# Attention trunk on one core: scores of two heads in one block with alternating row halves, dilated heads weighed in pairs

## The chip, the cores and the metric

One Trainium2 chip, one of its cores. The metric is device time in microseconds (us) of one execution. Engines in the views: PE is TensorE's matmul side, PEld its weight loads, DVE VectorE, ACT ScalarE, POOL GpSimd, SP SyncE, which issues the weights' DMAs. Names like L684 are lines of the kernel before; in the changed kernel the same lines lie one to three further down.

## The reference, cut to what matters

A decoder trunk of two layers over 256 positions of width 2048, all in fp32. Layer 0 mixes with sliding-window attention (job A, 16 heads) and with three dilated patterns that are merged per position (jobs B0 and B1, 4 heads each, three patterns a head); layer 1 with stick-breaking attention (jobs C0 and C1, 8 heads each) and latent attention (jobs D0 and D1, 8 heads each). An MLP of width 8192 follows in each layer.

```python
# A and B, per head (B: for each of three patterns)
scores = einsum(q, k) * (1 / sqrt(64)) - slope * distance     # masked
p = exp(scores - max(scores)); out = (p @ v) / sum(p)
# C, per head: strictly causal, no softmax
z = einsum(q, k) * scale
after = reverse_cumsum(log_keep) - log_keep
out = exp(log_beta + after) @ v
# D, per head: 64 + 32 = 96 numbers in q and k
s = (einsum(q_nope, k_nope) + einsum(q_rope, k_rope)) * scale
out = softmax(s) @ v
```

## The kernel before, in words

**Big matmuls.** All projections and MLP products run on PE with weights that stream from HBM in units of 128 x 1024 (`Stream`). Each unit is split into a high and a low part: ACT casts `w_hi` (L120), DVE subtracts to get `w_lo` (L121). Three units are split ahead of their use. `ws` (L325, L326) holds the weights in the array, `as_` (L371 to L373) the activations.

**Attention between them.** After each unit of weights `pump` runs one step of the attention (`attn_step`), so a step's small matmuls stand in PE's queue as one block between two runs of big ones. The order is written out: `todo` lists the scores still to be made, `due` what later steps must do, `flips` the transposes. In a step come first what is due (weighing, then the flip, then later stages), then one new score if the list and the buffers allow it.

One head of a job goes through these stages:

- *score* (step i): `qk` makes the scores of 256 positions in two matmuls, 128 x 128 (L684) and 128 x 256 (L685), into a PSUM tile `sc`, of which there are two, one bank each. A, B and C heads have 64 numbers, so q and k lie on 64 partitions: even heads on 0 to 63, odd ones on 64 to 127. D heads lie on partitions 0 to 95. In the same step the job's first stage runs on DVE and frees `sc`: bias and row maxima in A, B and D (L767, L808, L1024, then L699), the mask in C (L1043).
- *later stages*, a step apart: in A, B and D the exponentials on ACT and the division on DVE; in C three functions on ACT, sums on DVE (L1054, two scans L1057, L1058) and the exponential on ACT.
- *flip*: three transposes on PE (L259) and a copy to SBUF as `pT` on ACT, one head and pattern a step.
- *weigh*, two steps later: `v` times `pT` into the PSUM tile `o` (L278, L280). A head writes 64 of the 128 partitions of `o`, odd heads the upper half. In A, C and D two heads are weighed together, with their matmuls alternating; in B each head and pattern by itself. After both heads `y` is made on ACT and DVE (L284, L285).

Every job's heads are scored one a step, each pattern of B by itself, in a list that grows as the projections finish.

Of the kernel before, what the change touches and what calls it, by code (L numbers as in the profile page):

```python
# [11 lines left out]
F32 = mybir.dt.float32  # L12
# [6 lines left out]
P = 128  # L19
S = 256  # L20
# [143 lines left out]
class Trunk:  # L164
    def __init__(self, tc, ctx, args):
        self.tc = tc
        self.nc = tc.nc
        self.a = args
        self.split_ahead = 3
        self.dma_ahead = 5  # L170
        pool = lambda name, bufs, **kw: ctx.enter_context(tc.tile_pool(name=name, bufs=bufs, **kw))
        self.const = pool("const", 1)
        self.raw = pool("raw", 6)
        self.spl = pool("spl", 4)
        self.res = pool("res", 1)
        self.small = pool("small", 5)
        self.ps = pool("ps", 1, space=bass.MemoryType.PSUM)
        self.w = Stream(self)
        self.side = deque()
        self.late = deque()  # L180
        self.todo = deque()
        self.due = {}
        self.flips = deque()
        self.s_live = 0
        self.i = 0


    def pump(self):
# [15 lines left out]

    def queue(self, job, u=None):

        if u is None:
            self.todo.extend((job, h, 0) for h in range(job.n))
        else:
            self.todo.extend((job, h, u) for h in range(job.n))  # L210

    def at_step(self, i, prio, fn, *args):
        self.due.setdefault(i, []).append((prio, len(self.due.get(i, ())), fn, args))
# [1 line left out]
    def attn_step(self):  # L215
        i = self.i
        self.i += 1
        if self.flips and self.flips[0][0] <= i:
            _, job, h, u = self.flips.popleft()
            self.at_step(i, 2, self.flip, job, h, u)  # L220
            if job.per > 1:
                self.at_step(i + 2, 1, self.weigh, job, (h,), u)
            elif h % 2:
                self.at_step(i + 2, 1, self.weigh, job, (h - 1, h), 0)
        for _, _, fn, args in sorted(self.due.pop(i, []), key=lambda t: t[:2]):
            fn(*args)
        if not self.todo:
            return
        job, h, u = self.todo[0]
        per = job.per  # L230
        if h not in job.s:
            if self.s_live == self.s_bufs:
                return
            self.s_live += 1
            if per > 1:
                job.s[h] = self.at.tile([P, per * 384], F32, name="S", bufs=self.s_bufs)
            else:
                pair = self.at.tile([P, 768], F32, name="S", bufs=self.s_bufs)
                job.s[h], job.s[h + 1] = pair[:, 0:384], pair[:, 384:768]
        self.todo.popleft()  # L240
        sc = self.ps.tile([P, 384], F32, name="sc", bufs=2)
        job.score(h, u, sc)
        job.stages[0](h, u, sc, job.s[h])
        if u == per - 1:
            for n, fn in enumerate(job.stages[1:]):
                self.at_step(i + 1 + n, 3, fn, h, job.s[h])
            self.flips.extend((i + job.lag, job, h, v) for v in range(per))

    def finish(self, job):
        while job.left:  # L250
# [427 lines left out]
            one(t, 3, mv, r)  # L678


    def qk(self, sc, q, k):

        nc = self.nc
        nc.tensor.matmul(sc[:, 0:P], q[:, 0:P], k[:, 0:P], start=True, stop=True, skip_group_check=True)  # L684
        nc.tensor.matmul(sc[:, P:384], q[:, P:S], k, start=True, stop=True, skip_group_check=True)  # L685

    def softmax(self, per, scale=1.0, sink=None):

# [44 lines left out]
    def even(self):  # L733
        nc = self.nc
        slopes = alibi(16)
        qa = self.project(512, scale=0.125) + self.project(512, scale=0.125)
        kd = self.tile2()
        va = self.tile2()
        kvf = self.at.tile([P, 2, S], F32, name="kvf", bufs=1)
        vf = kvf[:, 1, :]  # L740

        def take(f, bank):
            self.join(kvf[:, f, :], bank)
            if f == 0:
                for kv in range(2):
                    for half in range(2):
                        eng = nc.scalar.copy if half else nc.vector.tensor_copy
                        eng(kd[half * HD:half * HD + HD, kv, :], kvf[kv * HD:kv * HD + HD, 0, :])

        self.ws(self.xT, KT, 256, take)  # L750
        self.pump()

        def flip_v():
            pt = self.ps.tile([P, 384], F32, name="pt")
            for t in range(2):
                nc.tensor.transpose(pt[:, t * P:(t + 1) * P], vf[:, t * P:(t + 1) * P], self.ident)
            nc.vector.tensor_copy(va[:, :, 0:P], pt[:, 0:S].rearrange("p (t c) -> p t c", t=2))

        self.at_step(self.i, 0, flip_v)
        top, power, divide = self.softmax(1, sink=lambda h: self.sinks[:, h:h + 1])  # L760

        def score(h, u, sc):
            r = slice((h % 2) * HD, (h % 2) * HD + HD)
            self.qk(sc, qa[h // 4][r, (h // 2) % 2, :], kd[r, h // 8, :])

        def bias(h, u, sc, st):
            nc.vector.scalar_tensor_tensor(st, self.masks[:, 0, :], -slopes[h], sc, op0=ALU.mult, op1=ALU.add)  # L767
            top(h, st)

        def value(h, u, blk):  # L770
            return va[:, blk, (h // 8) * HD:(h // 8) * HD + HD]

        ja = Job("A", 16, 1, score, (bias, power, divide), value, 5, self.y_at)
        self.queue(ja)
        jb = [self.even_b(0, self.y_at), self.even_b(1, self.x_slot)]
        self.finish(jb[0])
        self.finish_side()
        ys = ja.out + jb[0].out
        st = self.new_stats()

        def rest():
            self.finish(jb[1])
            yield jb[1].out

        late = LazyTiles(rest())
        late.tiles += ys
        for c in range(3):
            o = self.as_(late if c == 2 else ys, 12 if c == 2 else 10, 512)
            self.add_res(o, c, True, st if c == 2 else None)
            self.pump()  # L790
        for c in range(2):
            o = self.as_(jb[1].out, 2, 512)
            self.add_res(o, c, False, st)
        o = self.as_(late, 12, 512, hold=2)
        return (o, 3, True), st

    def even_b(self, half, y):
        nc = self.nc
        sl = alibi(8)
        qkv = []  # L800
        top, power, divide = self.softmax(3)

        def score(h, u, sc):
            r = slice((h % 2) * HD, (h % 2) * HD + HD)
            self.qk(sc, qkv[u][0][r, h // 2, :], qkv[u][1][r, h // 2, :])

        def bias(h, u, sc, st):
            nc.vector.scalar_tensor_tensor(st[:, u * 384:(u + 1) * 384], self.masks[:, 1 + u, :], -sl[half * 4 + h], sc,  # L808
                                           op0=ALU.mult, op1=ALU.add)
            if u == 2:  # L810
                top(h, st)

        def value(h, u, blk):
            return qkv[u][2][:, blk, h * HD:h * HD + HD]

        job = Job(f"B{half}", 4, 3, score, (bias, power, divide), value, 4, y)
        for gi in range(3):
            q = self.project(256, scale=0.125)[0]
            k = self.project(256)[0]
            qkv.append((q, k, None))  # L820
            self.queue(job, gi)
            o = self.as_(self.xT, KT, 256)
            v = self.tile2()
            for t in range(2):
                nc.scalar.copy(v[:, t, :], o[t])
            self.pump()
            qkv[gi] = (q, k, v)
        return job
# [186 lines left out]
    def job_d(self, name, qs, kv, y):  # L1015
        nc = self.nc
        ks, vs = kv
        top, power, divide = self.softmax(1, scale=1.0 / math.sqrt(96))

        def score(h, u, sc):  # L1020
            self.qk(sc, qs[h // 2][0:96, h % 2, :], ks[h // 2][0:96, h % 2, :])

        def bias(h, u, sc, st):
            nc.vector.tensor_tensor(st, self.masks[:, 1, :], sc, op=ALU.add)  # L1024
            top(h, st)

        def value(h, u, blk):
            return vs[h // 4][:, blk, (h % 4) * HD:(h % 4) * HD + HD]

        job = Job(name, 8, 1, score, (bias, power, divide), value, 5, y)  # L1030
        self.queue(job)
        return job

    def job_c(self, name, qs, ks, vs, y):
        nc = self.nc
        kept = {}

        def score(h, u, sc):
            r = slice((h % 2) * HD, (h % 2) * HD + HD)
            self.qk(sc, qs[h // 4][r, (h // 2) % 2, :], ks[h // 4][r, (h // 2) % 2, :])  # L1040

        def mask(h, u, sc, st):
            nc.vector.tensor_tensor(st, self.masks[:, 0, :], sc, op=ALU.add)  # L1043
# [22 lines left out]
        job = Job(name, 8, 1, score, (mask, soft, sums, power), value, 6, y)  # L1066
# [98 lines left out]
```

## Time and profile before

| | before |
|---|---|
| median of 3 runs | 2243.89 us (2241.61 to 2249.12) |
| the profiled execution | 2248.41 us, span 2246.6 us |
| PE busy | 2216.6 us (99%) |
| DVE busy | 1406.8 us (63%) |
| ACT busy | 1060.7 us (47%) |
| mean granted clock of TensorE | 0.996 |

A busy time is the union of an engine's instructions. PE's instructions overlap, so the distance between two starts tells what one of them costs the engine, not the duration of a row. An fp32 matmul appears as two passes, each with its own weight load.

### The profile page before, as it was taken

Reading aid. Unit: us, or ns where it says so; the run is one execution under the profiler, and the core shown is the slowest. Engines: PE = TensorE matmul, PEld = TensorE weight load, DVE = VectorE, ACT = ScalarE, POOL = GpSimd, SP = SyncE. Lnnn points to the kernel's source line nnn. Section 1 sums busy time; section 2 is a strip of 40 time slices with the busy share of each in tenths; the row PEclk is TensorE's granted clock in tenths of the full one; section 3 lists DMA queues with packets and bytes.
Section 4 is the critical chain, followed back from the end, with each engine's and each line's share of the span. In section 5 each row is a group of like instructions: output and inputs, shape, how many; then the busy total and the mean of one; then the engine's idle time right before and its main releaser. Section 6 shows DMA issues by size and latency. Waiting matters only on the chain.

```text
span 2246.6 us, 30036 instructions
## 1 busy us (share of the span) xinstructions
PE 2216.6 (99%) x11604; PEld 1847.6 (82%) x11604; DVE 1406.8 (63%) x1903; ACT 1060.7 (47%) x1525; POOL 62.0 (3%) x85
## 2 busy tenths in 40 slices
PE   9999999999999999999999999999999999999997
PEld 7878887788888888888878887778888888888885
DVE  5766355776556456556567887978555655554655
ACT  4554344454345345345344575635434534444542
POOL 0000000000000000000003201000000000000001
PEclk9999999999999999999999999999999999999998
DMA  7444454555655556565658443455656556555652
GB/s 266 145 118 147 131 168 141 189 178 193 191 187 188 190 176 200 193 188 170 206 161 226 154 136 127 148 184 184 227 194 189 178 198 189 186 194 181 194 190 104
DMA packets 224320, 399.07 MB, mean 178 GB/s; under 512 B 12778, under 2 KB 56512, under 8 KB 223408
## 3 DMA queue, kind: packets, MB, share of 16 engines
q1 hardware_dynamic: 221760, 387.30, 54.2%
q0 software_dynamic: 2416, 9.84, 1.6%
q8 instruction: 91, 1.49, 0.3%
q14 instruction: 53, 0.43, 0.1%
HBM read 395.00 MB, written 2.10 MB: 177 GB/s over the span
## 4 chain that ended last, share of the span: by engine, by line
PE 64%; issue 30%; DVE 4%; ACT 1%; DMA 1%; POOL 0%; SPq 0%; POOLq 0%; DVEq 0%; ACTq 0%
PE acc L325 14%; PE acc L371 9%; PE acc L373 9%; PE acc L372 9%; PE acc L326 7%; PE sc L325 3%; PE sc L326 2%; PE o L325 2%; PE pt L325 2%; PE pt L259 1%; PE o L278 1%; PE sc L685 1%; DVE w_lo L121 1%; PE sc L684 1%; PE o L326 1%
## 5 line engine op out<-in xcount | busy, mean ns | idle before, releaser
L121 DVE TENSOR_TENSOR w_lo<-raw,w_hi 128x1024 fp32r<-128x1024 f32 (+2 forms) x748 | 891.5, 1204 | 600.0 <-ACT w_hi L120 595.0
L120 ACT CAST w_hi<-raw 128x1024 fp32r<-128x1024 f32 (+2 forms) x748 | 759.9, 1029 | 770.2 <-PE acc L373 460.9
L325 PE MATMUL acc<-x,w_hi 128*128 128x512 f32 x1824 | 654.0, 402 | 4.3 <-DVE x L514 4.0
L326 PE MATMUL acc<-x,w_lo 128*128 128x256 f32 x1824 | 512.3, 281 | 0.6 <-DVE w_lo L121 0.6
L325 PEld LDWEIGHTS acc<-x,w_hi 128*128 128x128 f32 x1824 | 343.3, 188 | 94.4 <-issue 6.6
L373 PE MATMUL acc<-w_hi,h_lo 128*128 128x512 f32 x1016 | 400.3, 394 | 0.0
L372 PE MATMUL acc<-w_lo,h_hi 128*128 128x512 f32 x1016 | 398.2, 392 | 0.0
L371 PE MATMUL acc<-w_hi,h_hi 128*128 128x512 f32 x1016 | 394.4, 388 | 0.0
L326 PEld LDWEIGHTS acc<-x,w_lo 128*128 128x128 f32 x1824 | 345.2, 189 | 1.4 <-DVE w_lo L121 0.9
L372 PEld LDWEIGHTS acc<-w_lo,h_hi 128*128 128x128 f32 x1016 | 190.7, 188 | 44.3
L371 PEld LDWEIGHTS acc<-w_hi,h_hi 128*128 128x128 f32 x1016 | 190.7, 188 | 42.7
L373 PEld LDWEIGHTS acc<-w_hi,h_lo 128*128 128x128 f32 x1016 | 191.0, 188 | 38.1
L325 PE MATMUL sc<-x,w_hi 128*128 128x512 f32 x512 | 186.7, 399 | 0.0
L326 PE MATMUL sc<-x,w_lo 128*128 128x256 f32 x512 | 143.8, 281 | 0.0
L371 PE MATMUL acc<-w_hi,x 128*128 128x256 f32 (+2 forms) x400 | 136.4, 341 | 0.3 <-DVE x L513 0.2
L373 PE MATMUL acc<-w_hi,x 128*128 128x256 f32 (+2 forms) x400 | 132.5, 331 | 0.0
L372 PE MATMUL acc<-w_lo,x 128*128 128x256 f32 (+2 forms) x400 | 132.4, 331 | 0.0
L325 PEld LDWEIGHTS sc<-x,w_hi 128*128 128x128 f32 x512 | 96.2, 188 | 23.9
L337 ACT ACTIVATE xfull<-acc 128x256 f32<-128x256 f32 x130 | 49.6, 383 | 126.2 <-PE acc L326 108.7
L326 PEld LDWEIGHTS sc<-x,w_lo 128*128 128x128 f32 x512 | 96.7, 189 | 0.0
L325 PE MATMUL o<-x,w_hi 128*128 128x512 f32 x256 | 96.3, 399 | 0.0
L325 PE MATMUL pt<-x,w_hi 128*128 128x512 f32 x256 | 96.2, 399 | 0.0
(203 smaller groups left out, 2163.9 us busy)
## 6 DMA issues: line engine op xcount, KB each, us to landing
raw<-in_mlp_w SPq DMA_DIRECT2D x512, 512.0 KB, 4.2
raw<-in_even_w_in SPq DMA_DIRECT2D x92, 512.0 KB, 4.4
raw<-in_odd_w_in SPq DMA_DIRECT2D x56, 512.0 KB, 4.1
raw<-in_odd_w_out SPq DMA_DIRECT2D x32, 512.0 KB, 3.7
raw<-in_even_w_out SPq DMA_DIRECT2D x24, 512.0 KB, 3.7
gb_rows<-in_ln_g POOLq DMA_DIRECT2D x3, 1024.0 KB, 5.0
gb_rows<-in_ln_b POOLq DMA_DIRECT2D x3, 1024.0 KB, 7.1
raw<-in_odd_w_uq SPq DMA_DIRECT2D x8, 384.0 KB, 4.7
```

Source lines behind the costliest of these rows:

```text
L120: nc.scalar.copy(h, r)
L121: nc.vector.tensor_tensor(l, r, h.bitcast(F32), op=ALU.subtract)
L259: nc.tensor.transpose(pt[:, b * P:(b + 1) * P], st[:, u * 384 + b * P:u * 384 + (b + 1) * P], self.ident)
L278: nc.tensor.matmul(o[rows, :], v, w[:, 0:S], start=first, stop=False, skip_group_check=True)
L325: nc.tensor.matmul(banks[f], hi[:, c:c + P], both, start=first, stop=False, skip_group_check=True)
L326: nc.tensor.matmul(banks[f][:, S:2 * S], lo[:, c:c + P], xh, start=False, stop=last, skip_group_check=True)
L337: nc.scalar.activation(t, bank[:, S:2 * S], AF.Copy, scale=scale)
L371: nc.tensor.matmul(outs[t], xh[:, ts], hi[:, c:c + width], start=first, stop=False, skip_group_check=True)
L372: nc.tensor.matmul(outs[t], xh[:, ts], lo[:, c:c + width], start=False, stop=False, skip_group_check=True)
L373: nc.tensor.matmul(outs[t], xl[:, ts], hi[:, c:c + width], start=False, stop=last, skip_group_check=True)
L684: nc.tensor.matmul(sc[:, 0:P], q[:, 0:P], k[:, 0:P], start=True, stop=True, skip_group_check=True)
L685: nc.tensor.matmul(sc[:, P:384], q[:, P:S], k, start=True, stop=True, skip_group_check=True)
```

## The change

Scores are now made for a pair of heads (2k, 2k + 1) in one step; the next pair may come two steps later (`turn`). `qk` takes two score tiles and issues the two heads' matmuls in turn: 128 x 128 of the even head, of the odd head, then 128 x 256 of each. The first stage of both heads runs in this step, the later stages of the odd head one step after those of the even head, as before. In B the flips of a pair alternate, and each pattern is weighed for both heads together, as in the other jobs.

```diff
     def queue(self, job, u=None):
-        if u is None:
-            self.todo.extend((job, h, 0) for h in range(job.n))
-        else:
-            self.todo.extend((job, h, u) for h in range(job.n))
+        self.todo.extend((job, h, u or 0) for h in range(0, job.n, 2))
...
             self.at_step(i, 2, self.flip, job, h, u)
-            if job.per > 1:
-                self.at_step(i + 2, 1, self.weigh, job, (h,), u)
-            elif h % 2:
-                self.at_step(i + 2, 1, self.weigh, job, (h - 1, h), 0)
+            if h % 2:
+                self.at_step(i + 2, 1, self.weigh, job, (h - 1, h), u)
...
-        if not self.todo:
+        if not self.todo or i < self.turn:
             return
         job, h, u = self.todo[0]
-        per = job.per
+        per, pair = job.per, (h, h + 1)
         if h not in job.s:
-            if self.s_live == self.s_bufs:
+            need = 2 if per > 1 else 1
+            if self.s_live + need > self.s_bufs:
                 return
-            self.s_live += 1
+            self.s_live += need
...
         self.todo.popleft()
-        sc = self.ps.tile([P, 384], F32, name="sc", bufs=2)
-        job.score(h, u, sc)
-        job.stages[0](h, u, sc, job.s[h])
+        self.turn = i + 2
+        scs = [self.ps.tile([P, 384], F32, name="sc", bufs=2) for _ in pair]
+        self.qk(scs, [job.score(g, u) for g in pair])
+        for j, (g, sc) in enumerate(zip(pair, scs)):
+            job.stages[0](g, u, sc, job.s[g])
+            if u == per - 1:
+                for n, fn in enumerate(job.stages[1:]):
+                    self.at_step(i + j + 1 + n, 3, fn, g, job.s[g])
         if u == per - 1:
-            for n, fn in enumerate(job.stages[1:]):
-                self.at_step(i + 1 + n, 3, fn, h, job.s[h])
-            self.flips.extend((i + job.lag, job, h, v) for v in range(per))
+            self.flips.extend((i + j + job.lag, job, g, v) for v in range(per) for j, g in enumerate(pair))
...
-    def qk(self, sc, q, k):
-        nc = self.nc
-        nc.tensor.matmul(sc[:, 0:P], q[:, 0:P], k[:, 0:P], start=True, stop=True, skip_group_check=True)
-        nc.tensor.matmul(sc[:, P:384], q[:, P:S], k, start=True, stop=True, skip_group_check=True)
+    def qk(self, scs, qks):
+        nc = self.nc
+        for cols, qs, ks in ((slice(0, P), slice(0, P), slice(0, P)), (slice(P, 384), slice(P, S), slice(0, S))):
+            for sc, (q, k) in zip(scs, qks):
+                nc.tensor.matmul(sc[:, cols], q[:, qs], k[:, ks], start=True, stop=True, skip_group_check=True)
```

The score functions of the four jobs now return q and k in place of calling `qk`.

**Order on PE, scores of A** (two steps in the middle of the job). Before:

```order
L259 MATMUL pt<-ident,S 128x128 x3
L684 MATMUL sc<-qk 128x128
L685 MATMUL sc<-qk 128x256
...
L278 MATMUL o<-pT,qk 64x256 x2
L280 MATMUL o<-pT,qk 64x128 x2
L259 MATMUL pt<-ident,S 128x128 x3
L684 MATMUL sc<-qk 128x128
L685 MATMUL sc<-qk 128x256
```

Now:

```order
L260 MATMUL pt<-ident,S 128x128 x3
...
L279 MATMUL o<-pT,qk 64x256 x2
L281 MATMUL o<-pT,qk 64x128 x2
L260 MATMUL pt<-ident,S 128x128 x3
L688 MATMUL sc<-qk 128x128 x2
L688 MATMUL sc<-qk 128x256 x2
```

One of two steps has no score any more, the other has both (the big matmuls between are left out). Transposes and weighing stay at their steps.

**Order on PE, weighing of B1** (two steps beside the output projection; the three rows L371 to L373, later L372 to L374, come four times between two blocks). Before:

```order
L278 MATMUL o<-pT,qk 64x256
L280 MATMUL o<-pT,qk 64x128
L259 MATMUL pt<-ident,S 128x128 x3
L371 MATMUL acc<-w_hi,y 128x512
L372 MATMUL acc<-w_lo,y 128x512
L373 MATMUL acc<-w_hi,y 128x512
...
L278 MATMUL o<-pT,qk 64x256
L280 MATMUL o<-pT,qk 64x128
L259 MATMUL pt<-ident,S 128x128 x3
```

Now:

```order
L279 MATMUL o<-pT,qk 64x256 x2
L281 MATMUL o<-pT,qk 64x128 x2
L260 MATMUL pt<-ident,S 128x128 x3
L372 MATMUL acc<-w_hi,y 128x512
L373 MATMUL acc<-w_lo,y 128x512
L374 MATMUL acc<-w_hi,y 128x512
...
L260 MATMUL pt<-ident,S 128x128 x3
```

Every second step loses its weighing, and the other one weighs two heads. Over all of B, 10 of the weighings that go stood ahead of transposes, 2 had no transposes behind them.

**Order on DVE, C0** (from the sums of the first head on). Before:

```order
L1058 TENSOR_TENSOR S<-S,sb_a 128x384
L1043 TENSOR_TENSOR S<-masks,sc 128x384
L121 TENSOR_TENSOR w_lo<-raw,w_hi 128x1024
L1054 SCALAR_TENSOR_TENSOR sb_a<-S,sb_a 128x384
L1057 SCALAR_TENSOR_TENSOR sb_a<-sb_a 128x128
L1057 SCALAR_TENSOR_TENSOR sb_a<-sb_a 128x256
L1058 TENSOR_TENSOR S<-S,sb_a 128x384
L1043 TENSOR_TENSOR S<-masks,sc 128x384
L121 TENSOR_TENSOR w_lo<-raw,w_hi 128x1024
```

Now:

```order
L1061 TENSOR_TENSOR S<-S,sb_a 128x384
L1046 TENSOR_TENSOR S<-masks,sc 128x384 x2
L121 TENSOR_TENSOR w_lo<-raw,w_hi 128x1024
L1057 SCALAR_TENSOR_TENSOR sb_a<-S,sb_a 128x384
L1060 SCALAR_TENSOR_TENSOR sb_a<-sb_a 128x128
L1060 SCALAR_TENSOR_TENSOR sb_a<-sb_a 128x256
L1061 TENSOR_TENSOR S<-S,sb_a 128x384
L121 TENSOR_TENSOR w_lo<-raw,w_hi 128x1024
```

Two masks follow one another in every second step; the odd head's has moved ahead of one head's sums and one unit's split.

## Rows read from the trace of the kernel before

**Rows 1.** Waits of PE: line, waited for, us in total, times, longest us
```profile
PE sc L684 <- DVE S L1043: 2.4, 5, 1.1
...
PE acc L993 <- ACT c L897: 0.3, 1, 0.3
```
**Rows 2.** Timeline of PE, a score of B1: start us, us, engine line, out<-in, xcount
```profile
335.66 0.28 PE L372 MATMUL acc<-w_lo,x 128*128 128x256 f32 x1
335.78 0.28 PE L373 MATMUL acc<-w_hi,x 128*128 128x256 f32 x1
335.99 0.49 PE L684 MATMUL sc<-qk 64*128 64x128 f32 x2
...
337.06 0.28 PE L372 MATMUL acc<-w_lo,x 128*128 128x256 f32 x1
```
**Rows 3.** Timeline of PE, weighing of one head of B0
```profile
272.85 0.28 PE L326 MATMUL acc<-x,w_lo 128*128 128x256 f32 x1
...
273.19 0.28 PE L326 MATMUL acc<-x,w_lo 128*128 128x256 f32 x1
273.40 0.65 PE L278 MATMUL o<-pT,qk 128*64 128x256 f32 x2
...
274.54 0.28 PE L326 MATMUL acc<-x,w_lo 128*128 128x256 f32 x1
```
**Rows 4.** Timeline of PE, weighing of two heads of D0
```profile
1370.11 0.28 PE L326 MATMUL acc<-x,w_lo 128*128 128x256 f32 x1
1370.32 0.65 PE L278 MATMUL o<-pT,d 128*64 128x256 f32 x4
...
1371.46 0.28 PE L326 MATMUL acc<-x,w_lo 128*128 128x256 f32 x1
```
**Rows 5.** Timeline of PE, one head's weighing with transposes (228), transposes alone (1353)
```profile
228.40 0.28 PE L326 MATMUL acc<-x,w_lo 128*128 128x256 f32 x1
...
230.02 0.28 PE L326 MATMUL acc<-x,w_lo 128*128 128x256 f32 x1
...
1352.97 0.28 PE L967 MATMUL acc<-y,w_lo 128*128 128x256 f32 x1
...
1353.66 0.28 PE L326 MATMUL acc<-x,w_lo 128*128 128x256 f32 x1
```
**Rows 6.** Timeline of PE, score of a head of D0
```profile
1326.10 0.28 PE L326 MATMUL acc<-x,w_lo 128*128 128x256 f32 x1
1326.22 0.38 PE L684 MATMUL sc<-d 96*128 96x128 f32 x2
...
1327.11 0.27 PE L326 MATMUL acc<-x,w_lo 128*128 128x256 f32 x1
```
**Rows 7.** Busy us by stretch: length, PE, PEld, DVE, ACT, POOL, PEclk, DMA share, GB/s
```profile
74.00:348.00 274.00, 274.00 (x1706) 227.00 (x1705) 167.32 (x302) 128.68 (x255) 0.00 (x0) 1.00 0.47 141
1276.00:1316.00 40.00, 39.20 (x197) 29.42 (x198) 39.18 (x61) 31.31 (x60) 7.06 (x6) 1.00 0.43 127
1387.40:1453.40 66.00, 64.10 (x329) 49.24 (x331) 64.40 (x129) 47.03 (x101) 5.91 (x6) 1.00 0.37 120
```
**Rows 8.** Weight loads of a line: count, duration ns min/median/max, first and last start
```profile
L684 PEld LDWEIGHTS sc<-qk x80: 182/184/186, 74.6 to 343.9; 64*128 64x128 f32 x80
...
L278 PEld LDWEIGHTS o<-pT,qk x80: 132/134/137, 106.5 to 398.0; 128*64 128x64 f32 x80
```
**Rows 9.** Timeline of DVE, masks of the fourth and fifth head of C0
```profile
1290.21 0.55 DVE L1043 TENSOR_TENSOR S<-masks,sc 128x384 f32<-128x384 f32 x1
...
1293.92 0.55 DVE L1043 TENSOR_TENSOR S<-masks,sc 128x384 f32<-128x384 f32 x1
```
**Rows 10.** Timeline of PE, scores of the last two heads of C0
```profile
1294.95 0.49 PE L684 MATMUL sc<-c 64*128 64x128 f32 x2
...
1299.08 0.48 PE L684 MATMUL sc<-c 64*128 64x128 f32 x2
```
**Rows 11.** Timeline of PE, score of the fifth head of C0, with idle time and releaser
```profile
1286.70 0.48 PE L684 MATMUL sc<-c 64*128 64x128 f32 x2 [0.20 <-DVE S L1043]
```

More of the change, by code (lines that the diff above doesn't have):

```diff
@@ L185, in __init__ @@
         self.i = 0
+        self.turn = 0
     def pump(self):
@@ L228, in attn_step @@
             return
         job, h, u = self.todo[0]
-        per = job.per
+        per, pair = job.per, (h, h + 1)
         if h not in job.s:
-            if self.s_live == self.s_bufs:
+            need = 2 if per > 1 else 1
+            if self.s_live + need > self.s_bufs:
                 return
-            self.s_live += 1
+            self.s_live += need
             if per > 1:
-                job.s[h] = self.at.tile([P, per * 384], F32, name="S", bufs=self.s_bufs)
-            else:
-                pair = self.at.tile([P, 768], F32, name="S", bufs=self.s_bufs)
-                job.s[h], job.s[h + 1] = pair[:, 0:384], pair[:, 384:768]
+                for g in pair:
+                    job.s[g] = self.at.tile([P, per * 384], F32, name="S", bufs=self.s_bufs)
+            else:
+                both = self.at.tile([P, 768], F32, name="S", bufs=self.s_bufs)
+                job.s[h], job.s[h + 1] = both[:, 0:384], both[:, 384:768]
@@ L760, in even, with score @@
         top, power, divide = self.softmax(1, sink=lambda h: self.sinks[:, h:h + 1])
-        def score(h, u, sc):
+        def score(h, u):
             r = slice((h % 2) * HD, (h % 2) * HD + HD)
-            self.qk(sc, qa[h // 4][r, (h // 2) % 2, :], kd[r, h // 8, :])
+            return qa[h // 4][r, (h // 2) % 2, :], kd[r, h // 8, :]
         def bias(h, u, sc, st):
@@ L801, in even_b, with score @@
         top, power, divide = self.softmax(3)
-        def score(h, u, sc):
+        def score(h, u):
             r = slice((h % 2) * HD, (h % 2) * HD + HD)
-            self.qk(sc, qkv[u][0][r, h // 2, :], qkv[u][1][r, h // 2, :])
+            return qkv[u][0][r, h // 2, :], qkv[u][1][r, h // 2, :]
         def bias(h, u, sc, st):
@@ L1018, in job_d, with score @@
         top, power, divide = self.softmax(1, scale=1.0 / math.sqrt(96))
-        def score(h, u, sc):
-            self.qk(sc, qs[h // 2][0:96, h % 2, :], ks[h // 2][0:96, h % 2, :])
+        def score(h, u):
+            return qs[h // 2][0:96, h % 2, :], ks[h // 2][0:96, h % 2, :]
         def bias(h, u, sc, st):
@@ L1036, in job_c, with score @@
         kept = {}
-        def score(h, u, sc):
+        def score(h, u):
             r = slice((h % 2) * HD, (h % 2) * HD + HD)
-            self.qk(sc, qs[h // 4][r, (h // 2) % 2, :], ks[h // 4][r, (h // 2) % 2, :])
+            return qs[h // 4][r, (h // 2) % 2, :], ks[h // 4][r, (h // 2) % 2, :]
         def mask(h, u, sc, st):
```

## The prediction, made before the change ran

> **What bounds the kernel now.** The share of each engine comes first: TensorE (PE) is busy nearly all of the span, no other engine is. The table of waits then says how little PE waits for others: in the attention, most for the scores (L684) to VectorE's mask (DVE, L1043), 2.4 us in all, and once 0.3 for ScalarE [rows 1]. So PE's own instructions set the time wherever no such wait stands, and what an attention step costs is what its block of small matmuls adds between the big ones. That is read in the timeline of PE: start of the last big matmul ahead of a block, start of the second big matmul behind it, less the two distances that stand there without a block. Each fp32 matmul of the program shows as two passes.
>
> - Score of one head with 64 rows: 335.78 to 337.06 is 1.28 us; two big matmuls of this kind take 2 x 0.12 [rows 2]. The block costs **1.04 to 1.05**.
> - Weighing of one head: 273.19 to 274.54 is 1.35, less 0.35: **1.00** [rows 3].
> - Weighing of two heads together, eight passes in place of four: 1370.11 to 1371.46 is 1.35 again, **1.00** [rows 4]. The two heads write different halves of PSUM's partitions, and the second costs nothing: passes on two halves of the array's columns run at the same time.
> - Weighing of one head ahead of three transposes: 228.40 to 230.02 is 1.62; transposes alone, 1352.97 to 1353.66, 0.69 [rows 5]. The weighing adds 0.93.
> - Score of one head of job D, 96 rows: 1326.10 to 1327.11 is 1.01, less 0.35: **0.66** [rows 6]. The same four passes cost 0.39 less than with 64 rows: with all rows in use nothing is drained at the block's two ends.
>
> Then the busy time by stretch [rows 7]: in layer 0's attention (74 to 348) DVE works 167.3 of 274 us, 61%; in layer 1 there are two stretches, 1276 to 1316 and 1387.4 to 1453.4, where it works 39.2 of 40 and 64.4 of 66, 98%. There PE and DVE are nearly level, and a PE made faster meets DVE.
>
> **The change, part by part.** The profiled execution took 2248.4 us, 4.5 above the median 2243.9; what is summed below comes off either.
>
> *Weighing of the dilated heads (B).* 24 single weighings become 12 of two heads. Of the 12 that go, by the order of PE's instructions, 10 stood ahead of transposes and 2 alone: 10 x 0.93 + 2 x 1.00 = **11.3 us**. The price of a pair is measured in this very kernel [rows 4], so this term is nearly certain. No engine waits for it: the same pT tiles are copied at the same steps.
>
> *Scores of A and B.* 16 and 24 single blocks become 8 and 12 blocks of two heads. The heads of a pair lie on rows 0 to 63 and 64 to 127 of the array and write two PSUM banks. No row of the trace shows two row halves at work together, so the price of a pair is bounded: from below 1.05 (all under cover, as with column halves), from above, on one array setting, 1.05 + 0.66 = 1.71 (one behind the other, without a second pair of ends). I take 1.05, since the nearest row is the weighing of two [rows 4]: passes of 64-wide tiles that share no output. Saved: 20 x 1.05 = **21.0 us**. Weight loads could cut into that: a load of 128 columns shows 184 ns, one of 64 columns 134, so 50 ns more for 64 columns [rows 8]. Eight loads at about 0.10 are 0.80 against the 0.66 of streaming; a pair would cost 1.19 and the term shrink by 20 x 0.14 = 2.8.
>
> The Trainium skill, TensorE: Matmul & The Clock Gate, "Part 3: Packing small matmuls", lists four row tiles at 3.07 times one, not 4. As an estimate by that ratio a pair's streaming would be 0.66 x 4 / 3.07 = 0.86, the term 4 us smaller and the time 2215; no run here shows it.
>
> What hides the DVE side in layer 0: bias and maxima of two heads now stand in one step, none in the next. With 21.0 + 11.3 off 274 us DVE's 167.3 are 69% of the stretch. A pair waits for the biases of the pair before, two steps back, and the work that stands ahead of those on DVE is one bias and its maxima more than before. I cost it at nothing; if DVE falls behind, PE waits at the scores, some tenths of a us at each.
>
> *Scores of C.* By the same price 8 x 1.05 = 8.4 would go. But here DVE is full. For one step's work it takes 3.71 (mask at 1290.21, the next at 1293.92 [rows 9]); PE's step with a score is 4.13 [rows 10], and without every second score 4.13 - 0.52 = 3.61, less than DVE's. Already before, the fifth score waited 0.20 for the mask of the third head [rows 11]. After the change the third pair waits for the masks of the second, one mask (0.55) later: 1287.2 in place of 1286.7. The fourth pair waits for the mask that began at 1293.92 and the one behind it, so until 1295.0, and the old score of that head began at 1294.95 [rows 10]. Up to there nothing is gained; the score left out a step later gives 1.05, and the next stop, where PE already waits 0.3 for ScalarE's copies of v [rows 1], takes most of it back, since those copies stand behind work that DVE feeds. The second group (C1 and then D1) stays at 98% of DVE to its end, so it gains less. I take **0.5 us** for all of C. The bounds: 8.4 + 2.4 = 10.8 if DVE keeps up, minus 1 if the longer wait for two masks costs at each pair. The Trainium skill, TensorEngine Tiling (Array Packing), "Performance Considerations", says that tiling speeds up TensorE but not the emptying of PSUM; held against every job it would deny the 21.0 too, while the 61% in layer 0 [rows 7] speak against that.
>
> *Scores of D.* 96 rows fill more than half the array; two heads in one block cost 2 x 0.66 as before: **0**. *The rest* (the turn counter, the pair's buffers) is Python that leaves no instruction. The last weighing of B and of D stands at the same big matmul in both orders, so no attention step is left uncovered at a stage's end.
>
> Sum: 11.3 + 21.0 + 0.5 = 32.8. **2243.9 - 32.8 = 2211.1**, say 2211 (2215.6 in the profiled execution).
>
> **Rivals.**
> 1. *The row halves only partly overlap.* Loads or fills bind, a pair costs 1.19 to 1.25: 2214 to 2215. For it the longer loads [rows 8]; against it the column halves, which lose nothing [rows 4].
> 2. *The row halves don't overlap.* A pair costs 1.71 and saves 2.10 - 1.71 = 0.39: 20 x 0.39 + 11.3 + 0.5 = 19.6, so 2224. Nothing in the trace excludes it.
> 3. *Layer 1 gains too.* DVE's queue would have to give way, by the order in which masks and sums stand; then C's 8.4 and the waits' 2.4 come on top of the first two terms: 2243.9 - 43.1 = 2201. Against it the 98% [rows 7].
> 4. *Slower: each change of row half drains the array.* If the passes alternate between the heads, as the weighing's do, a pair has seven changes inside. The two ends of a block cost 0.39 together, so 0.20 a change: the pair is 0.39 + 8 x 0.165 + 7 x 0.20 = 3.1 against 2.10, and with all 28 pairs of 64 rows on PE's path the time is 2243.9 + 28 x 1.0 - 11.3 = 2261. It decides from a pair of 2.10 + 11.3 / 28 = 2.50 on, 0.11 a change. The weighing, which alternates column halves at no cost [rows 4], speaks against it.
>
> That the change doesn't do what it says (scores not in pairs) is excluded by the order of PE's instructions.
>
> **Numbers.** Forecast 0.54, rival 1 0.15, rival 2 0.14, rival 3 0.10, rival 4 0.04; 0.03 for a DVE that falls behind in layer 0 or a lower clock in longer waits. The range takes in rival 1, rival 2 and nearly rival 3: 2202 to 2226. A change within 0.3% (6.7 us, about what a measurement of this kernel can tell from none) would need a pair that costs 2.36 us or more, or the last case: 0.03; slower is rival 4, 0.04; faster is the forecast and rivals 1 to 3, 0.93.
>
> **What would show it.** Right: the block of a pair of A or B scores takes 1.05 us, its two heads' passes start within some ns of each other; weighings of B show eight passes in 1.00; PE's waits for DVE's masks of C grow from 2.4 to some 8 us or more, while the two stretches in layer 1 [rows 7] stay as long as they are. Wrong: a pair at 1.7 or over, or PE waiting for DVE at the scores of layer 0, or C's pairs passing without longer waits.

## The result, and the profile after

The changed kernel takes **2214.10 us** (median of 4 runs, 2212.65 to 2215.03), the kernel before on the same chip 2243.55 (4 runs, 2241.61 to 2249.12). The ratio is **0.9863, 95% interval 0.9849 to 0.9877**: 29.4 us less. The forecast was 2211, its range 2202 to 2226.

The profiled execution after took 2213.81 us with a span of 2212.0. The one before lay 4.9 us above its median, so the two spans differ by 34.6, more than the two medians do. What the traces show is therefore counted by stretches of their own. The page's busy time of each engine after:

```profile
PE 2177.3 (98%) x11603; PEld 1829.7 (83%) x11604; DVE 1403.4 (63%) x1903; ACT 1058.6 (48%) x1525; POOL 61.0 (3%) x85
```

Busy time by stretch after, for about the same big matmuls as those of [rows 7] (bounds, length, PE, PEld, DVE, ACT, POOL, granted clock, DMA share, GB/s):

```profile
74.40:322.70 248.30, 248.30 (x1704) 213.85 (x1703) 163.30 (x299) 128.08 (x255) 0.00 (x0) 1.00 0.49 153
1242.30:1282.30 40.00, 36.99 (x193) 28.53 (x192) 38.59 (x61) 31.21 (x60) 6.00 (x6) 0.96 0.43 130
1353.70:1419.70 66.00, 61.31 (x318) 46.91 (x317) 63.85 (x128) 46.52 (x102) 5.91 (x6) 1.00 0.34 120
```

In layer 0 PE is busy without a gap as before, and DVE's 163 of 248 us are 66%: PE still sets the time. In layer 1 DVE works 97% of both stretches, nearly as before, but PE only 92 to 93%. The same is seen in 214 us around all of layer 1's attention, from 1.5 us ahead of its first score on, in the same view; here is the kernel before, then the one after:

```profile
1269.70:1483.70 214.00, 211.30 (x1145) 166.88 (x1144) 181.21 (x332) 134.82 (x279) 15.53 (x14) 1.00 0.44 138
```
```profile
1236.00:1450.00 214.00, 206.31 (x1143) 164.53 (x1142) 180.39 (x332) 133.15 (x278) 14.47 (x14) 0.99 0.42 138
```

PE has 5.0 us less to do there and ends no earlier. From the start of the first score to the start of the last weighing, layer 0 takes 323.9 us before and 292.7 after (-31.2), layer 1 203.3 and 203.8 (+0.5). That sum, -30.7, is what the change did in the traces; the medians' 29.4 differ from it by less than the runs of one kernel differ among themselves (2.4 us after, 7.5 before).

**A pair of scores of A.** Timeline of PE after: start us, us, line, operands, count.

```profile
81.23 0.40 PE L326 MATMUL acc<-x,w_hi 128*128 128x512 f32 x1
81.46 0.28 PE L327 MATMUL acc<-x,w_lo 128*128 128x256 f32 x1
81.67 0.93 PE L688 MATMUL sc<-qk 64*128 64x128 f32 x8
82.53 0.50 PE L326 MATMUL acc<-x,w_hi 128*128 128x512 f32 x1
82.86 0.28 PE L327 MATMUL acc<-x,w_lo 128*128 128x256 f32 x1
```

From 81.46 to 82.86 it is 1.40; less the 0.35 of the two big matmuls the block costs **1.05**, the price of one head before [rows 2], and now it holds eight passes in place of four. Undisturbed pairs of A, B and C lie between 1.05 and 1.06. The single passes of the two heads start about 7 ns apart, in four couples: 81.673 and 81.680, 81.886 and 81.893, 81.998 and 82.005, 82.216 and 82.223.

**A weighing of two heads of B0**, to be held against [rows 3, 4]:

```profile
251.86 0.28 PE L327 MATMUL acc<-x,w_lo 128*128 128x256 f32 x1
252.06 0.65 PE L279 MATMUL o<-pT,qk 128*64 128x256 f32 x4
252.55 0.39 PE L281 MATMUL o<-pT,qk 128*64 128x128 f32 x4
252.87 0.50 PE L326 MATMUL acc<-x,w_hi 128*128 128x512 f32 x1
253.20 0.28 PE L327 MATMUL acc<-x,w_lo 128*128 128x256 f32 x1
```

1.34 less 0.35 is 0.99, for two heads what one cost before.

**Waits of PE after** (line, waited for, us in total, times, longest us), to be held against [rows 1]:

```profile
PE sc L688 <- DVE S L1046: 4.6, 3, 2.3
...
PE acc L373 <- DVE w_lo L121: 1.5, 1, 1.5
...
PE acc L996 <- ACT c L900: 0.7, 1, 0.7
PE sc L688 <- DVE S L1027: 0.6, 1, 0.6
```

The waits for DVE's masks of C grew from 2.4 to 4.6, one for D's masks and one of 1.5 for a unit's split have come, and the one for ScalarE grew from 0.3 to 0.7. All of them lie in layer 1. Scores of A and B wait for nothing that is long enough to appear.

The table holds idle time ahead of a row alone. Where a pair of C waits, its odd head's passes wait some 0.46 us more for their own mask, in the middle of the block: such a row is 1.39 long in place of 0.93 (below). Counted as the prediction prices blocks, three of the eight pairs wait, and the waits at C's scores, by the cost of the blocks over undisturbed ones, grew from 2.7 to 6.3 us.

**The third pair of C0.** First the score of the first head in the kernel before; then the timeline of PE after (in brackets the idle time ahead and what ended it), then that of DVE:

```profile
1271.19 0.48 PE L684 MATMUL sc<-c 64*128 64x128 f32 x2
```
```profile
1237.50 0.93 PE L688 MATMUL sc<-c 64*128 64x128 f32 x8
...
1253.00 1.39 PE L688 MATMUL sc<-c 64*128 64x128 f32 x8 [2.28 <-DVE S L1046]
1254.31 0.50 PE L372 MATMUL acc<-w_hi,x 128*128 128x512 f32 x1
```
```profile
1248.02 0.68 DVE L958 TENSOR_TENSOR d<-d,rope_f 32x512 f32<-32x512 f32 x1
1248.73 0.56 DVE L1057 SCALAR_TENSOR_TENSOR sb_a<-S,sb_a 128x384 f32<-128x384 f32 x1
1249.33 2.33 DVE L1060 TENSOR_TENSOR_SCAN sb_a<-sb_a 128x128 f32<-128x128 f32 x2
1251.70 0.78 DVE L1061 TENSOR_TENSOR S<-S,sb_a 128x384 f32<-128x384 f32 x1
1252.40 1.00 DVE L1046 TENSOR_TENSOR S<-masks,sc 128x384 f32<-128x384 f32 x2
```

DVE runs without a gap up to the two masks that PE waits for. The fifth head of C0 was scored 15.5 us after the first one before (1271.19 to 1286.70 [rows 11]), and is scored 15.5 us after it now (1237.50 to 1253.00). What PE saves in two pairs, 2.1 us, it spends waiting for the third. The pair's first head needs only the first of the two masks.

### The profile page after: what moved, and what is told of

Read it like the earlier page. It is cut to its first block, busy times and chain, and to the rows that moved or that the text cites. A ratio compares the mean times of both kernels' runs of the same rounds, so it can differ in the third digit from the quotient of the medians.

```text
span 2212.0 us, 30040 instructions
## 1 busy us (share of the span) xinstructions
PE 2177.3 (98%) x11603; PEld 1829.7 (83%) x11604; DVE 1403.4 (63%) x1903; ACT 1058.6 (48%) x1525; POOL 61.0 (3%) x85
## 4 chain that ended last, share of the span: by engine, by line
PE 61%; issue 31%; DVE 5%; DMA 1%; ACT 1%; POOL 0%; SPq 0%; POOLq 0%; DVEq 0%; ACTq 0%
PE acc L326 14%; PE acc L372 9%; PE acc L374 9%; PE acc L373 9%; PE acc L327 7%; PE sc L326 3%; DVE w_lo L121 2%; PE sc L327 1%; PE o L326 1%; PE pt L326 1%; PE sc L688 1%; PE pt L260 1%; PE o L279 1%; DMA raw<-in_even_w_in 1%; PE o L327 1%
## 5 line engine op out<-in xcount | busy, mean ns | idle before, releaser
L374 PE MATMUL acc<-w_hi,h_lo 128*128 128x512 f32 x1016 | 398.5, 392 | 0.0
L373 PE MATMUL acc<-w_lo,h_hi 128*128 128x512 f32 x1016 | 398.2, 392 | 0.0
L372 PE MATMUL acc<-w_hi,h_hi 128*128 128x512 f32 x1016 | 396.1, 390 | 0.0
L372 PEld LDWEIGHTS acc<-w_hi,h_hi 128*128 128x128 f32 x1016 | 190.7, 188 | 42.6
L373 PEld LDWEIGHTS acc<-w_lo,h_hi 128*128 128x128 f32 x1016 | 190.8, 188 | 42.4
L374 PEld LDWEIGHTS acc<-w_hi,h_lo 128*128 128x128 f32 x1016 | 190.9, 188 | 40.0
L372 PE MATMUL acc<-w_hi,x 128*128 128x256 f32 (+2 forms) x400 | 136.3, 341 | 0.3 <-DVE x L514 0.2
L374 PE MATMUL acc<-w_hi,x 128*128 128x256 f32 (+2 forms) x400 | 133.2, 333 | 0.0
L373 PE MATMUL acc<-w_lo,x 128*128 128x256 f32 (+2 forms) x400 | 133.0, 332 | 0.1
```

Of the source, the lines that this page charges most:

```text
L372: nc.tensor.matmul(outs[t], xh[:, ts], hi[:, c:c + width], start=first, stop=False, skip_group_check=True)
L373: nc.tensor.matmul(outs[t], xh[:, ts], lo[:, c:c + width], start=False, stop=False, skip_group_check=True)
L374: nc.tensor.matmul(outs[t], xl[:, ts], hi[:, c:c + width], start=False, stop=last, skip_group_check=True)
```

## The experiments

The theory was that the gain is layer 0's alone: the row halves overlap there, the weighing costs nothing for the second head, and layer 1 gives nothing because DVE holds it. Each run is compared with the kernel before on the same chip (2246.44 for the first four, 2244.63 for the next four, 2246.65 for the last four; 2243.55 beside the changed kernel). Medians of different groups are therefore best held against each other by their ratios.

### Both heads on the same rows

```diff
-        self.qk(scs, [job.score(g, u) for g in pair])
+        self.qk(scs, [job.score(h, u) if job.rows64 else job.score(g, u) for g in pair])
```

> The odd head's score is made from the even head's q and k (in A, B and C), so both heads' passes use the same 64 rows; the odd heads' scores are left out of the result. Theory (the two row halves work at the same time): a pair's block in layer 0 grows from 1.05 to about 1.71 us, 20 x 0.66 = 13.2 us in all, about 2227; C adds nothing, since DVE covers it. Rival (the gain came from having half as many blocks, not from overlap): the block stays as it is, 2214. Rival (each change of half or bank costs): shorter than 2214.

Measured: 2230.6, ratio 0.9930 (0.9915 to 0.9945), so 16.6 us over the next run, which differs from the changed kernel only in the order of the matmuls.

```profile
82.28 0.28 PE L328 MATMUL acc<-x,w_lo 128*128 128x256 f32 x1
82.49 1.57 PE L689 MATMUL sc<-qk 64*128 64x128 f32 x8
83.99 0.49 PE L327 MATMUL acc<-x,w_hi 128*128 128x512 f32 x1
84.33 0.28 PE L328 MATMUL acc<-x,w_lo 128*128 128x256 f32 x1
```

2.05 less 0.35 is 1.70: with the same instructions, the same two banks and the same alternation, but one row half, a pair costs what the prediction bounded it by from above (1.71). The passes now start one after the other, at 82.489, 82.703, 82.814 and so on. So the 0.65 of the second head is hidden by the row halves and by nothing else. 20 pairs by 0.65 are 13.0; layer 0 grows by 12.2 (292.9 to 305.1), layer 1 by 3.4. The expectation had put layer 1 at nothing, since DVE would cover it, and that was a miss: C's blocks with their waits cost 3.4 us more than in the next run, so DVE's pace covers only part of the longer pairs. Why stays open.

### One head's matmuls, then the other's

```diff
-        for cols, qs, ks in (...):
-            for sc, (q, k) in zip(scs, qks):
+        for sc, (q, k) in zip(scs, qks):
+            for cols, qs, ks in (...):
```

> A pair's matmuls in the order even head 128 and 256 columns, then odd head 128 and 256 columns, instead of alternating. Theory 1 (PE starts passes strictly in the order of the program): only the last pass of the even head and the first of the odd head overlap, a block is about 1.05 + 0.66 - 0.11 = 1.60 us, 20 x 0.55 = 11 us more, 2225. Theory 2 (a pass for the free half starts ahead of one that waits for its own half): no change, 2214.

Measured: 2214.02, ratio 0.9861 (0.9844 to 0.9877): no change.

```profile
81.40 0.28 PE L327 MATMUL acc<-x,w_lo 128*128 128x256 f32 x1
81.61 0.93 PE L688 MATMUL sc<-qk 64*128 64x128 f32 x8
82.47 0.51 PE L326 MATMUL acc<-x,w_hi 128*128 128x512 f32 x1
82.81 0.28 PE L327 MATMUL acc<-x,w_lo 128*128 128x256 f32 x1
```

1.41 less 0.35 is 1.06. The alternation, which the change writes out, isn't needed: the passes still start in couples, now 13 to 14 ns apart (81.605 and 81.619). The second head's first pass starts ahead of the first head's later ones.

### B weighed one head at a time

```diff
-            if h % 2:
+            if job.per > 1:
+                self.at_step(i + 2, 1, self.weigh, job, (h,), u)
+            elif h % 2:
                 self.at_step(i + 2, 1, self.weigh, job, (h - 1, h), u)
```

> B's heads are weighed one by one again, everything else as changed. Theory: 12 more blocks of 0.93 to 1.00 us, 11.3 us more, about 2225.5. Rival (the pairs of weighings only move PE's time to a wait elsewhere): 2214 to 2218.

Measured: 2225.4, ratio 0.9909 (0.9895 to 0.9924), 11.4 us over the run above, which weighs two heads together. Layer 0 grows from 292.9 to 303.8. This term of the sum stands at its size.

### C and D scored one head a step

```diff
-        self.todo.extend((job, h, u or 0) for h in range(0, job.n, 2))
+        self.todo.extend((job, h, u or 0) for h in range(0, job.n, job.step))
...
-        per, pair = job.per, (h, h + 1)
+        per, pair = job.per, (h, h + 1)[:job.step]
...
-        self.turn = i + 2
+        self.turn = i + job.step
```

`step` is 1 for the jobs C and D, else 2.

> The scores of C and D one head a step as before the change, A and B in pairs. Theory (DVE sets the pace in layer 1's attention): within 1 us of the changed kernel, 2213 to 2215, with PE's waits for DVE's masks back at about 2.5 us in place of 5.2. Rival 1 (the pairs of C do give 8 x 1.05): 2222. Rival 2 (the longer wait for two masks costs more than it gives): 2211 to 2213.

Measured: 2212.53, ratio 0.9854 (0.9839 to 0.9868). Layer 1 takes 203.3 us (203.8 with pairs), and the waits for C's masks are back at what they were:

```profile
PE sc L690 <- DVE S L1048: 2.3, 5, 1.1
```

Pairs in layer 1 give nothing. Whether they cost something is not settled: 1.5 us between medians and 0.5 in the trace are within what runs differ by.

### C without its two scans, before and after

In both kernels the same line goes:

```diff
-                nc.vector.tensor_tensor_scan(r, r, r, 0.0, ALU.add, ALU.bypass)
+                pass
```

The kernel before:

> The kernel before without the two scans of C (the reverse sums are left out, so C's result isn't the reference's): 32 scans less on DVE, 18.8 us in all, in the two stretches where DVE worked 98%. Both theories: a few us faster than before, at least the 2.4 us of PE's waits for masks, so 2239 to 2243. It is the partner of the next run.

The changed kernel:

> The changed kernel without the same scans. Theory (C's pairs gave nothing because DVE was full): with DVE relieved the pairs of C give most of their 8 x 1.05, so this run is 37 to 41 us faster than its partner, 2200 to 2205, against 29.4 between the changed kernel and the one before. Rival (C's pairs cost as much elsewhere as they save, whatever DVE does): the difference stays at 29 to 32 us, about 2210.

Measured: 2240.73 (0.9983, 0.9974 to 0.9993) and 2204.13 (0.9822, 0.9807 to 0.9836), **36.6 us** apart where the kernels with scans were 29.4 apart. Layer 1 takes 200.0 and 195.0, so the pairs now gain 5.0 us there, and layer 0 gains 31.2 as ever. (The 29.4 and the 36.6 were not measured beside each other; the 5.0 is from the traces, where the kernels with scans have -0.5.) Without the scans, which take 18.8 us of DVE in C, PE waits little for C's masks in the changed kernel:

```profile
PE sc L688 <- DVE S L1046: 0.8, 2, 0.6
```

That is the cause of the missing gain, shown by taking the load away: the pairs are as cheap in C as in A, but DVE held what they save. The scans are also a link in each head's chain of stages, so these two runs alone don't tell DVE's load from the chain's length; that DVE works without a gap up to the masks that PE waits for (above) speaks for the load. Not all of C's 8.4 came, even so.

### Work moved from DVE and POOL to ScalarE

First the rotary part of D's k (a copy on POOL), then also DVE's copies of k and v behind C and D:

```diff
-            nc.gpsimd.tensor_copy(k[64:96], ...)
+            nc.scalar.copy(k[64:96], ...)
```

> The changed kernel with the eight copies of the shared rotary key (32 x 512) on ACT instead of POOL. In the stretches where DVE is full, DVE's instructions last longer while POOL works (a split 1.8 instead of 1.2 us). Theory (DVE's time sets the pace there): 1 to 3 us faster, 2211 to 2213. Rival (ACT is the next bound): no change or slower by the eight copies, some 4 us.

```diff
-            copy = nc.vector.tensor_copy if f > 1 else nc.scalar.copy
+            copy = nc.scalar.copy
...
-                (nc.vector.tensor_copy if t else nc.scalar.copy)(v[:, t, :], ...)
+                nc.scalar.copy(v[:, t, :], ...)
```

> As the run before, and the six copies of k and v that DVE makes in each of the two ukv (0.41 us each, 5 us in all) go to ACT too. Theory (DVE sets the pace): faster still, 2208 to 2211. Rival (ACT, whose copies free PE's accumulators there, is late): PE's wait for ACT's copies grows and the time is that of the run before or above.

Measured: 2212.38 (0.9859, 0.9843 to 0.9876) and 2214.6 (0.9866, 0.9851 to 0.9881). The first can't be told from the changed kernel. Its long splits stay, 1.79 and 1.90 us in the two stretches: they stand beside another instruction of POOL (L959, a sum in D's rotary part) that the run leaves there. The second is a miss for the theory: DVE has less to do (173 of 214 us, 180 in the changed kernel), and no time is gained; in the trace layer 1 is longer (206.4). Its waits of PE, then the 214 us around layer 1's attention:

```profile
PE acc L372 <- ACT d L1007: 2.7, 2, 1.8
...
PE acc L326 <- ACT d L1007: 1.8, 1, 1.8
PE sc L688 <- DVE S L1046: 1.7, 1, 1.7
```
```profile
1236.00:1450.00 214.00, 206.65 (x1132) 164.36 (x1131) 172.84 (x319) 141.19 (x298) 8.33 (x6) 0.97 0.41 136
```

The waits for masks fell from 4.6 to 1.7, and in their place stand 4.5 us for copies that now queue on ScalarE. All waits of PE in this attention together are no longer than in the changed kernel (7.4 and 7.7 us), so the waits changed their name, and the work taken from the full engine bought nothing. That layer 1 is 2.6 us longer in this trace isn't theirs to explain: more of it runs at the lower clock (0.97 granted over the 214 us, 0.99 in the changed kernel; on this see the last section).

### C's softplus as one logarithm

`ln(1 + exp z)` in place of `max(z, 0) + ln(1 + exp(-|z|))`, so without the guard for large z: one function less on ScalarE and one instruction less on DVE for each head.

```diff
-            nc.scalar.activation(a, st, AF.Abs)
-            nc.scalar.activation(a, a, AF.Exp, scale=-1.0)
+            nc.scalar.activation(a, st, AF.Exp)
...
-            nc.vector.scalar_tensor_tensor(a, st, 0.0, a, op0=ALU.max, op1=ALU.add)
```

> The changed kernel with C's softplus made as ln(1 + exp(z)) by two functions on ACT, in place of max(z, 0) + ln(1 + exp(-|z|)) by three on ACT and one on DVE: 16 instructions of 0.55 us (8.8 us) less on DVE, 16 of 0.52 (8.4 us) less on ACT, both in the stretches where DVE is full. The output stays the reference's as long as no score is above some 80. Theory (DVE sets the pace of C): about half of what the 18.8 us less of the run without scans gave, which was 10 us: 2207 to 2210. Rival (ACT's chain sets it): no more than 2 us.

Measured: 2210.24, ratio 0.9836 (0.9822 to 0.9849). The expectation, 2207 to 2210, is missed by 0.2. Layer 1 takes 197.1 us, 6.7 less than in the changed kernel, for 16 x 0.55 = 8.8 us of DVE that went. PE waits for masks twice, 2.7 us in all. Over the same 214 us, which now hold more than the attention, PE is again as busy as in the kernel before, and DVE less:

```profile
1236.00:1450.00 214.00, 211.29 (x1175) 170.10 (x1174) 177.14 (x323) 128.84 (x266) 15.84 (x14) 0.99 0.46 143
```

This agrees with the light runs, in a kernel that leaves no sums out: relieve DVE in C, and time comes back. By itself it proves less, since ScalarE was relieved by as much (8.4 us), and the kernel before was not run with one logarithm, so how much of the 6.7 the pairs gave isn't known.

Two more runs build on it: the copy of the rotary part on ScalarE again, then also D's scores one head a step (`step` is 1 for D alone).

> As the run before, and the copies of the rotary key on ACT instead of POOL. Theory: another 1 to 2 us, 2205 to 2209, as alone. Rival (with DVE relieved POOL no longer matters, and the copies burden ACT, on whose copies PE waited 1.4 us): the same as the run before or 1 to 2 us slower.

> As the run before, with D's scores one head a step again, C's in pairs. Theory (D's pairs give nothing on PE and make the next pair wait for two biases): 1 to 2 us faster. Rival (it is C's pairs that cost the 1.6 us of the run with single scores in C and D): no change.

Measured: 2209.92 (0.9841, 0.9827 to 0.9854), no further gain; and 2208.34 (0.9832, 0.9819 to 0.9846), the lowest median of a kernel that leaves no sums out, 38.3 us under the kernel before. All three beat both kernels by their medians, but can't be told from each other: layer 1 is 197.1, 196.6 and 196.7 long.

Last, D's scores one a step without any of these, with C's in pairs:

> The changed kernel with D's scores one head a step, C's in pairs. The run with both single was 1.6 us faster than the changed kernel. Theory (D's pairs make the waits): all of it returns, 2212 to 2213. Rival (C's pairs cost it): 2214.

Measured: 2215.82 (0.9862, 0.9849 to 0.9876). That is 30.8 under the kernel before on the same chip, where the changed kernel lay 29.4 under it. No gain that can be told from none; D's pairs cost nothing that can be seen.

## Why the prediction was right

**Weighing of B, 11.3 us: right.** 11.4 by the run without it. The price was in the trace before [rows 4], and nothing else depended on the step.

**Scores of A and B, 21.0 us: right.** The one price that no row showed, two row halves at work together, was taken from the nearest row, the column halves, and is 1.05 to 1.06. Summed over PE's blocks of attention in layer 0 the cost went from some 86 to 54 us, 32.1 less against the 32.3 of the first two terms. The attention's length in layer 0 fell by 31.2. The rest stands at no block and no wait: the distances of the other big matmuls, some 1300 of them, add up to 0.8 us more than before, under 1 ns each. Why stays open.

- *Rival 1* (1.19 to 1.25 a pair) is out by the 1.05. A load still shows about the same time as before (median 187 ns, [rows 8]: 184), and eight of them don't lengthen the block.
- *Rival 2* (1.71) is what happens on one row half, not on two; the price was worked out rightly for the case that didn't come.
- *Rival 4* (a drain at each change of row half) would need 0.11 us a change. None can be seen: eight passes take the time of four, in either order.
- The Trainium skill, TensorE: Matmul & The Clock Gate, "Part 3: Packing small matmuls", gives four row tiles 3.07 times the speed of one. As an estimate by that ratio a pair was 0.86 of streaming where the trace shows 0.66 to 0.67; for two tiles of 64 rows the loss that it implies isn't seen here.

**DVE in layer 0, nothing: right.** Its share has risen from 61 to 66% and PE doesn't wait for it at a score. The prediction's 69% took the whole 32.3 off this stretch; 25.7 of the 31.2 fell into it.

**Scores of C, 0.5 us: right in mechanism, a little too high.** Layer 1 is 0.5 longer in the trace and not measurably different in the runs. DVE's pace sets it: 15.5 us to the fifth head in both kernels. The stops were where the prediction had them (the third pair at the second pair's masks, then ScalarE's copies, 0.3 to 0.7), but not all of them, and not at their sizes. The third pair was worked out to start one mask later than before; its first head starts as before, and only the odd head one mask later. The waits at C's scores came to 6.3 us, not to 8 or more. By the cost of the blocks and the distances of the big matmuls the 8.4 that the pairs save go like this: 3.6 more in the waits at C's scores, 1.1 in D's, 1.5 for a split that DVE made late, 0.6 for ScalarE's copies, and 1.6 in big matmuls at a lower clock behind a wait (last section). D's waits and the late split were not forecast, the lower clock only as part of a chance of 0.03. So it is in part luck that the 0.5 came out within 1 us; that layer 1 gains next to nothing is not.

- *Rival 3* (layer 1 gains too) is out, for the reason given, DVE's 98% [rows 7]; the light runs show that it would have come in part with DVE relieved, 5.0 of 8.4 us.
- The Trainium skill, TensorEngine Tiling (Array Packing), "Performance Considerations", says that tiling speeds up TensorE but not the emptying of PSUM, which may become the bottleneck. Layer 1 agrees (DVE 97%, the waits at L1046); in layer 0 it did not become one (DVE 66%, 31 us gained).

**Scores of D, 0: right** by the run with D alone changed back (2215.82, no gain).

The sum is 32.8, the medians are 29.4 apart, the traces show 30.7: about 1 us of the difference is layer 1, 1 the rest of layer 0, and what is left lies within the spread of the runs.

## What to carry to other kernels

Two fp32 matmuls that use half of the array's rows, one on each half and into different banks, cost what one costs in this kernel (1.05 us for eight passes as for four), so pairing heads of width 64 for the scores was worth a full block each time where TensorE set the time. Before such a pairing is priced, read the share of the engine that empties PSUM stage by stage: at 61% the whole saving came, at 98% nothing did, and only less work on that engine set some of it free. Work moved from it to another engine that TensorE waits for bought nothing here: the wait only changed its name.

## What the runs showed of the hardware that was not expected

**Passes on the free row half start early.** With one head's four passes issued ahead of the other's, the passes still start in couples, 13 to 14 ns apart in place of 7, and the time is the same (2214.02 and 2214.10). The change had written the alternation out, and theory 1 of that run gave it a part in the overlap.

**Behind a wait of PE the granted clock can fall.** In the kernel before the clock of layer 1's attention is 1.00 throughout. In the changed kernel it falls after the 2.28 us of waiting ahead of the third pair of C0, and the big matmuls that otherwise follow each other at 0.23 us do so at 0.43, as at 1.2 GHz in place of 2.4. Stretches of 4 us (columns as above), then PE's timeline:

```profile
1250.00:1254.00 4.00, 1.72 (x11) 1.07 (x10) 3.97 (x6) 1.45 (x3) 3.51 (x5) 1.00 0.19 79
1254.00:1258.00 4.00, 4.00 (x13) 2.92 (x11) 3.93 (x7) 2.77 (x6) 0.00 (x0) 0.61 0.48 131
1258.00:1262.00 4.00, 4.00 (x21) 3.09 (x19) 3.93 (x8) 3.66 (x8) 0.00 (x0) 0.96 0.44 131
```
```profile
1255.29 0.63 PE L372 MATMUL acc<-w_hi,x 128*128 128x512 f32 x1
1255.72 0.63 PE L373 MATMUL acc<-w_lo,x 128*128 128x512 f32 x1
...
1258.52 0.39 PE L374 MATMUL acc<-w_hi,x 128*128 128x512 f32 x1
1258.75 0.40 PE L372 MATMUL acc<-w_hi,x 128*128 128x512 f32 x1
```

Eight matmuls by 0.20 are some 1.6 us of PE. It doesn't follow every wait: in the changed kernel none falls after the 1.79 ahead of C1's third pair, while with one head's matmuls ahead of the other's the clock keeps 1.00 after 2.27 us in C0 and falls after 1.80 in C1, and with the one logarithm after 1.31. What decides between them stays open. What it costs the kernel isn't settled either: where the clock kept 1.00 in C0 the fourth pair started 22.9 us after the first, where it fell 24.4, and yet layer 1 is nearly as long (203.4 and 203.8). DVE, not PE, is full in these stretches (3.93 of 4 us); no run here has such a fall in a stage that TensorE bounds.
